# The next-to-last head's weights joined and split ahead of later casts, and loads reordered at two places of the output projection

## The chip, the cores and the metric

The kernel runs on one core of one Trainium2 chip. The metric is the device time of one execution in microseconds (us). The time before is 2003.12 us, the median of three runs (2003.05 to 2004.46).

## The reference

One block of a streaming encoder on 512 tokens of width 2048, all in float32. The input is normalised and projected; eight heads of stick-breaking attention and eight of forgetting attention follow; their normalised outputs go through `w_out` onto the residual, and then through a squared-ReLU layer of width 8192:

```python
h = rmsnorm(x, g_attn[l])
proj = jnp.einsum('bsd,de->bse', h, w_in[l])
...
o_sb = stick_breaking_attention(qa, ka, va)
o_fox = forgetting_attention(qf, kf, vf, log_f)
mixed = jnp.concatenate([head_rmsnorm(o_sb, g_out_sb[l]),
                         head_rmsnorm(o_fox, g_out_fox[l])], axis=-1)
x = x + jnp.einsum('bse,ed->bsd', mixed, w_out[l])
h2 = rmsnorm(x, g_mlp[l])
u = jax.nn.relu(jnp.einsum('bsd,df->bsf', h2, w_up[l]))
x = x + jnp.einsum('bsf,fd->bsd', u * u, w_down[l])
return rmsnorm(x, g_final)
```

Stick-breaking attention weighs key s for query t with `exp(log_beta + rest)`, where `rest` is a reversed running sum of `log_keep` along the keys.

## The kernel before

**Split operands.** Every float32 operand of a product is split in a high half (a cast to fp32r on ScalarE: `wh`, `hi`, `ph`, `g..H`) and a low half (source minus high half, on VectorE: `wl`, `lo`, `pl`). A product of two operands is three matmuls (`mm3`, lines 78 to 80): high times high, high times low, low times high. So each piece of weights that TensorE uses has been loaded (a DMA on SyncE's queue, SP), cast (ScalarE) and subtracted (VectorE). The raw pieces (`wraw`, `wo`) live in three buffers and the halves (`wh`, `wl`) in three more, `wx` in one more for a while (tile `px`). A load waits for the buffer that the low half of an earlier piece frees.

**Large products in seven.** The projection by `w_out`, like the others, is made of seven products of half the size, numbered 1 to 7, of sums and differences of blocks (`a_source`, line 1329, and `WeightSums`, line 1025, which writes those sums to DRAM as `wsums`, `wraws` and `whigh`). The second output block of stick-breaking heads is computed early, while the last head is still at work (class `Second`, line 1136).

**The attention's plan.** Up to line 1282 the order on TensorE, ScalarE and VectorE is written by hand: `plan.at(time, function)` collects steps, and `plan.run()` issues them in order of the planned time. The time is only a sorting key: each engine works its own list in order and waits where an operand is missing. The heads pass through a chain. For a stick-breaking head `plan_sb` (line 868) plans `start`, `soft`, `maxed`, `scan` (a running sum along the keys on VectorE, and the subtraction behind it, line 887) and `weights` (the exponential, line 890). The weights of all heads but the last are then turned by a DMA transpose (`halves` and `turn_halves`, lines 939 to 945), joined again (`join_halves`, line 947, on ScalarE, `pt`), and split (`t_high`, line 951, `ph`; `t_low`, line 955, `pl`) for the head's product with the values (`o`, line 965). The last head's weights are turned on TensorE (`turn`, line 931). The numbers for the next-to-last head stand in line 1260, those of the last head's scan in line 894, those of the pieces of `Second` in lines 1225 and 1226.

**The output projection.** From line 1594 on no times are given. The program is written piece by piece (`out_piece(p, db, m0)`: product p, column block db, rows m0 and m0 + 1), and the recording layer sorts the instructions of all engines by a simulated timeline; `with tc.issue_after(ins)` keeps what is written under it behind an instruction that it names. Around the change, in block 0, product 1 and product 4 come first (`accoa`, `accob`), then 5 (`accoc`), 6 (`accoa` again), 3 (`accoc` again) and 7 (`accoa`). When a product is complete, `take` (line 1547) adds it from PSUM to quarters of the residual (`x`, loaded by `begin`, line 1543); a complete quarter is stored (`xd`), transposed on TensorE (`turn_quarter`, line 1567, `tr`) and scaled by ScalarE into `hr` (line 1565). From `hr`, `left_form` (line 1588) makes the left operands `f` of the next layer, each with its sum on VectorE (lines 1335 to 1341), its cast and its low half. `hr` of column block 1 takes the buffers of block 0, so it is written once the forms of block 0 have been read. `pending` is the list of forms to come, one behind each piece.

Product 6's pieces load both halves ready-made (`whigh` and `wsums`, lines 1515 and 1516). Its last piece uses `wx`, the extra buffer. The loads for product 3's second piece, and the next quarter of the residual, are kept behind `behind`, a load of product 6 (lines 1632 and 1652).

Of the kernel before, what the change touches and what calls it, by code (L numbers as in the profile page):

```python
# [38 lines left out]
def block_kernel(ctx, tc, x, g_attn, w_in, b_f, g_out_sb, g_out_fox, w_out, g_mlp, w_up, w_down, g_final, y):  # L39
# [726 lines left out]
    with tc.tile_pool(name="att", bufs=1, side="right", reuse_waits="tile") as at, \  # L766
# [78 lines left out]
        class Head:  # L845
# [22 lines left out]
            def plan_sb(self, plan, t):  # L868
                g = self.h

                def start():
                    self.w = wide("w")
                    act.activation(self.w, self.s, AF.Abs)

                def soft():
                    act.activation(self.w, self.w, AF.Exp, scale=-1.0)
                    act.activation(self.w, self.w, AF.Ln, bias=1.0)

                def maxed():
                    dve.scalar_tensor_tensor(self.w, self.s, 0.0, self.w, op0=ALU.max, op1=ALU.add)  # L880
                    causal(self.w, ALU.is_gt, 0.0)

                def scan():
                    for r in rows(self.w):

                        dve.tensor_tensor_scan(r[:, ::-1], r[:, ::-1], r[:, ::-1], 0.0, op0=ALU.add, op1=ALU.max)
                    dve.tensor_tensor(self.w, self.s, self.w, op=ALU.subtract)

                def weights():
                    act.activation(self.w, self.w, AF.Exp)  # L890
                    causal(self.w, ALU.is_gt, 0.0)

                last_ = self.i == 2 * NH - 1
                for dt, f in zip((6.4, 7.7, 10.2, 14.5, 19.2) if last_ else (9.8, 11.0, 13.6, 17.0, 22.0), (start, soft, maxed, scan, weights)):
                    plan.at(t + dt, f)

            def plan_fox(self, plan, t):
# [52 lines left out]

            def t_high(self):
                self.ph, self.pl = wide("ph", F32R), wide("pl", F32R)
                act.copy(self.ph, self.pt)

            def t_low(self):
                dve.tensor_tensor(self.pl, self.pt, self.ph.bitcast(F32), op=ALU.subtract)
# [209 lines left out]
            sp.dma_start(second_x[db], xq[:, :2, db * NT:(db + 1) * NT])  # L1166

        def take_second(db, t):
            dve.tensor_tensor(second_x[db][:, t, :], second_x[db][:, t, :], second_ps[db][t], op=ALU.add)

        TRI, TPER = 0.681, 26.05
        heads = [Head(i) for i in range(2 * NH)]
# [7 lines left out]
        for n in range(2 * NH + 1):  # L1180
# [34 lines left out]
            else:  # L1215
# [4 lines left out]
                for db in range(2):  # L1220
                    for n0, m0 in enumerate((4, 6, 0, 2)):
                        w = Second(db, m0)
                        if db:
                            plan.at(t + (-10.0, -9.0, -8.0, 6.0)[n0], w.load)
                            plan.at(t + (3.4, 4.5, 10.3, 11.35)[n0], w.cast_apart if n0 < 2 else w.cast, *((n0,) if n0 < 2 else ()))
                            plan.at(t + (4.6, 7.0, 11.75, 12.95)[n0], w.low)
                        else:
                            plan.at(t + (-11.0, -5.5, -1.4, -1.35)[n0], w.load_parts)
                        for tt in range(2):
                            plan.at(t + at_unit16(unit), w.multiply, tt)  # L1230
                            unit += 1
# [25 lines left out]
            if 0 <= i_o < 2 * NH - 1:  # L1257
                H = heads[i_o]
                last_ = i_o == 2 * NH - 2
                for dt, f in zip((12.4, 15.5, 19.3) if last_ else (5.4, 8.5, 9.8), (H.join_halves, H.t_high, H.t_low)):  # L1260
                    plan.at(t + dt, f)
                if last_:
                    continue
# [331 lines left out]
    for db in range(2):  # L1595
# [3 lines left out]
        else:  # L1599
# [11 lines left out]
                out_piece(1, 0, 4)  # L1611
            begin(1, 0, 0)
            with tc.issue_after(last_heads[1].ins):
                for m0 in (0, 2, 4, 6):
                    ins = out_piece(4, 0, m0)
            for p in (1, 5):
                g_form(p, (6, 7), (7, 8))
# [5 lines left out]
        for p in (1, 5, 6, 3, 7, 4)[:6 if db else 5]:  # L1623
            for m0 in () if db == 0 and p == 1 else (0, 2, 4, 6):
# [22 lines left out]
                if (db or p in (3, 7, 4)) and m0 in (2, 6) and first_loads:  # L1647

                    with tc.issue_after(ins.ins):
                        u, k, a = first_loads.pop(0)  # L1650
                        units[u].load(k, a)
                if db == 0 and p == 6 and m0 == 4:
                    behind = ins

                    with tc.issue_after(ins.ins):
# [17 lines left out]
            if db == 1 or p != 1:  # L1673
                take(p, db)
            if db == 1:
                pending += [(q, 0, j) for q in {1: (4, 5, 6), 6: (2, 7, 3)}.get(p, ()) for j in range(2)]
            if len(squares) > 0:

                with ExitStack() as order_:
# [596 lines left out]
```

## Time and profile before

| what | value |
|---|---|
| median of three runs | 2003.12 us (2003.05 to 2004.46) |
| the profiled execution | 2002.29 us |
| its span, first to last instruction | 2000.6 us |
| TensorE busy | 99% of the span |
| VectorE busy | 88% |
| ScalarE busy | 60% |
| granted TensorE clock, mean | 0.999 |

The profile is of one execution, and times within it are in us from the start of its span. Busy time of TensorE is modelled, since matmuls overlap: the step from one 512-column matmul to the next is shorter than the duration that stands in its row. A row of the timeline gives the start, the duration, the engine (PE is TensorE, DVE VectorE, ACT ScalarE, POOL GpSimd, SPq SyncE's queue of DMA issues), the line, the operation, what it writes and reads, and in brackets the time that its engine sat idle before it, with the instruction that ended the wait. For a DMA the row is its issue; when it lands is told apart.

### The profile page before, as it was taken

To read this page: it belongs to the slowest core of one execution; us is meant where nothing else is said; L and a number is where in the kernel's file an instruction comes from. 1 tells how busy PE (TensorE), PEld (TensorE's weight loads), DVE (VectorE), ACT (ScalarE), POOL (GpSimd) and SP (SyncE) were. 2 spreads that over 40 slices of the span, in tenths; PEclk is the share of its full clock that TensorE was granted. 3 is DMA by queue.
4 is the path that set the end of the run, shared out by engine and by line. 5 is a ranking of instruction groups with operands and counts; after the bars stand their busy time and mean duration, and the time that the engine had idled before them with its cause. 6 is when DMAs were issued, how large, how long until landed. Compare 5 with 4: busy or idle time off the path is not lost.

```text
span 2000.6 us, 26669 instructions
## 1 busy us (share of the span) xinstructions
PE 1989.1 (99%) x10096; PEld 1708.7 (85%) x10096; DVE 1754.5 (88%) x1992; ACT 1205.0 (60%) x1636; POOL 63.1 (3%) x73
## 2 busy tenths in 40 slices
PE   9999999999999999999999999999999999999998
PEld 9988888888888889888888888888888888888887
DVE  7876888888888688999999999998898888988896
ACT  7544666778775565767677676766543444344344
POOL 0000011110110000000000000000000000000003
PEclk9999999999999999999999999999999999999999
DMA  7346977677786962666666666666694674674642
GB/s 258 126 146 203 285 247 232 201 227 222 218 295 223 325 216 95 200 207 197 220 187 211 203 197 203 199 212 232 243 351 166 231 270 145 238 271 162 217 161 85
DMA packets 309072, 426.66 MB, mean 213 GB/s; under 512 B 49440, under 2 KB 198736, under 8 KB 302416
## 3 DMA queue, kind: packets, MB, share of 16 engines
q1 hardware_dynamic: 307920, 422.33, 63.7%
q10 hardware_dynamic: 1024, 2.63, 0.3%
q8 instruction: 79, 1.29, 0.2%
q14 instruction: 49, 0.40, 0.1%
HBM read 318.07 MB, written 97.01 MB: 207 GB/s over the span
## 4 chain that ended last, share of the span: by engine, by line
PE 97%; DMA 1%; DVE 1%; issue 0%; ACT 0%; SPq 0%; DVEq 0%; ACTq 0%
PE psa L1415 11%; PE accd L79 8%; PE accd L80 8%; PE accd L78 8%; PE accq L78 6%; PE accq L79 6%; PE accq L80 6%; PE psa L1413 6%; PE psc L1415 5%; PE psc L1413 3%; PE psb L1415 3%; PE psb L1413 1%; PE m L79 1%; PE m L78 1%; PE m L80 1%; PE vy L79 1%
## 5 line engine op out<-in xcount | busy, mean ns | idle before, releaser
L2062 ACT CAST wh<-wd 128x1024 fp32r<-128x1024 f32 x126 | 125.0, 999 | 168.3 <-PE accd L80 58.2
L1948 DVE TENSOR_TENSOR wl<-wu,wh 128x1024 fp32r<-128x1024 f32 x157 | 191.4, 1220 | 13.4 <-ACT wh L1942 13.4
L78 PE MATMUL accq<-hH,wh 128*128 128x512 f32 x512 | 200.3, 391 | 0.0
L79 PE MATMUL accq<-hL,wh 128*128 128x512 f32 x512 | 199.4, 389 | 0.0
L80 PE MATMUL accq<-hH,wl 128*128 128x512 f32 x512 | 199.3, 389 | 0.0
L1942 ACT CAST wh<-wu 128x1024 fp32r<-128x1024 f32 x157 | 166.3, 1060 | 48.7 <-PE psc L1415 22.9
L1415 PE MATMUL psa<-f,wh 128*128 128x512 f32 x712 | 177.1, 391 | 0.0
L79 PE MATMUL accd<-wl,uf 128*128 128x512 f32 x436 | 169.6, 389 | 0.0
L80 PE MATMUL accd<-wh,uf 128*128 128x512 f32 x436 | 169.6, 389 | 0.0
L78 PE MATMUL accd<-wh,uf 128*128 128x512 f32 x436 | 169.4, 389 | 0.0
L2069 DVE TENSOR_TENSOR wl<-wd,wh 128x1024 fp32r<-128x1024 f32 x126 | 144.1, 1152 | 11.5 <-ACT wh L2062 11.5
L1415 PEld LDWEIGHTS psa<-f,wh 128*128 128x128 f32 x712 | 130.8, 188 | 25.3
L2062 ACT CAST wx<-wd 128x1024 fp32r<-128x1024 f32 (+1 forms) x82 | 80.8, 995 | 107.1 <-PE accd L80 43.5
L1783 DVE TENSOR_TENSOR m<-m,accd 128x1024 f32<-128x1024 f32 x84 | 102.3, 1218 | 47.4 <-PE accd L80 47.4
L80 PEld LDWEIGHTS accq<-hH,wl 128*128 128x128 f32 x512 | 96.1, 188 | 20.3
L78 PEld LDWEIGHTS accq<-hH,wh 128*128 128x128 f32 x512 | 96.2, 188 | 19.0
L79 PEld LDWEIGHTS accq<-hL,wh 128*128 128x128 f32 x512 | 96.2, 188 | 18.9
L78 PE MATMUL accd<-wx,uf 128*128 128x512 f32 x284 | 110.5, 389 | 0.0
L79 PE MATMUL accd<-wx,uf 128*128 128x512 f32 x284 | 110.5, 389 | 0.0
L80 PE MATMUL accd<-wx,uf 128*128 128x512 f32 x284 | 110.5, 389 | 0.0
L1413 PEld LDWEIGHTS psa<-f,wl 128*128 128x128 f32 x712 | 94.8, 191 | 5.2
L1413 PE MATMUL psa<-f,wl 128*128 128x256 f32 x712 | 97.2, 282 | 0.0
(498 smaller groups left out, 5069.3 us busy)
## 6 DMA issues: line engine op xcount, KB each, us to landing
wu<-in_w_up_dram SPq DMA_DIRECT2D x60, 1024.0 KB, 6.5
ufd<-st SPq DMA_DIRECT2D x98, 512.0 KB, 3.6
wd<-in_w_down_dram SPq DMA_DIRECT2D x48, 1024.0 KB, 8.4
uf<-ufd SPq DMA_DIRECT2D x42, 1024.0 KB, 6.6
wraw<-in_w_in_dram SPq DMA_DIRECT2D x64, 512.0 KB, 6.0
wo<-wsums SPq DMA_DIRECT2D x28, 512.0 KB, 4.8
wd<-in_w_down_dram SPq DMA_DIRECT2D x16, 768.0 KB, 8.0
uf<-ufd SPq DMA_DIRECT2D x14, 768.0 KB, 4.5
```

The lines of the kernel that those rows point to most:

```text
L78: pe.matmul(out, sh, mh, start=first, stop=False, skip_group_check=True)
L79: pe.matmul(out, sh, ml, start=False, stop=False, skip_group_check=True)
L80: return pe.matmul(out, sl, mh, start=False, stop=last, skip_group_check=True)
L1413: ins = pe.matmul(ps[:, 2 * P:], lo[:, a, :], f_parts(p, a)[0], start=False, stop=last, skip_group_check=True)
L1415: ins = pe.matmul(ps, hi[:, a, :], f_both(p, a), start=a == PAIRS[0] and p in (1, 5), stop=last, skip_group_check=True)
L1783: dve.tensor_tensor(M[p][:, :, db, :], M[p][:, :, db, :], ps, op=ALU.add)
L1942: act.copy(rooms[k][0], srcs[k])
L1948: lows[0] = dve.tensor_tensor(lo, srcs.pop(k), hi.bitcast(F32), op=ALU.subtract)
L2062: act.copy(rooms[k + 3][0], srcs[k + 3])
L2069: dve.tensor_tensor(rooms[k + 2][1], srcs.pop(k + 2), rooms[k + 2][0].bitcast(F32), op=ALU.subtract)
```

## The change

There are four parts; instructions are only moved, none is added or taken away.

1. In the attention's plan the subtraction behind the scan becomes a step of its own (`less`), which for the last head comes later than the scan (18.5 instead of 14.5). The next-to-last head's join, cast and low half come earlier (11.0, 14.0, 18.2 in place of 12.4, 15.5, 19.3). The cast and the low half of the last piece of `Second` come later (14.7 and 18.9 in place of 11.35 and 12.95).
2. The first piece of product 4 (`out_piece(4, 0, 0)`) is kept behind the next-to-last head's cast and behind the last `take_second` of block 0.
3. `behind` is the load of product 6's piece m0 = 6 instead of m0 = 4, so the quarter of the residual and product 3's second weights are loaded after product 6's last piece.
4. In the list of forms `(3, 0)` and `(7, 1)` change places.

```diff
                     for r in rows(self.w):
                         dve.tensor_tensor_scan(r[:, ::-1], r[:, ::-1], r[:, ::-1], 0.0, op0=ALU.add, op1=ALU.max)
+
+                def less():
                     dve.tensor_tensor(self.w, self.s, self.w, op=ALU.subtract)
...
-                for dt, f in zip((6.4, 7.7, 10.2, 14.5, 19.2) if last_ else (9.8, 11.0, 13.6, 17.0, 22.0), (start, soft, maxed, scan, weights)):
+                for dt, f in zip((6.4, 7.7, 10.2, 14.5, 18.5, 19.2) if last_ else (9.8, 11.0, 13.6, 17.0, 17.0, 22.0), (start, soft, maxed, scan, less, weights)):
                     plan.at(t + dt, f)
...
-                            plan.at(t + (3.4, 4.5, 10.3, 11.35)[n0], w.cast_apart if n0 < 2 else w.cast, *((n0,) if n0 < 2 else ()))
-                            plan.at(t + (4.6, 7.0, 11.75, 12.95)[n0], w.low)
+                            plan.at(t + (3.4, 4.5, 10.3, 14.7)[n0], w.cast_apart if n0 < 2 else w.cast, *((n0,) if n0 < 2 else ()))
+                            plan.at(t + (4.6, 7.0, 11.75, 18.9)[n0], w.low)
...
-                for dt, f in zip((12.4, 15.5, 19.3) if last_ else (5.4, 8.5, 9.8), (H.join_halves, H.t_high, H.t_low)):
+                for dt, f in zip((11.0, 14.0, 18.2) if last_ else (5.4, 8.5, 9.8), (H.join_halves, H.t_high, H.t_low)):
...
-                for m0 in (0, 2, 4, 6):
+                with tc.issue_after(now["t_high"].ins), tc.issue_after(now["second", 0].ins):
+                    out_piece(4, 0, 0)
+                for m0 in (2, 4, 6):
                     ins = out_piece(4, 0, m0)
...
-                if db == 0 and p == 6 and m0 == 4:
+                if db == 0 and p == 6 and m0 == 6:
                     behind = ins
...
-                pending += [(q, 0, j) for q in {1: (4, 5, 6), 6: (2, 7, 3)}.get(p, ()) for j in range(2)]
+                pending += {1: [(q, 0, j) for q in (4, 5, 6) for j in range(2)], 6: [(q, 0, j) for q, j in ((2, 0), (2, 1), (7, 0), (3, 0), (7, 1), (3, 1))]}.get(p, [])
```

(`now["t_high"]` and `now["second", db]` only record the two instructions that part 2 names.) Lines behind the first part move by two, those behind the third by four, in the changed kernel.

**Where the instructions stand.** VectorE at the end of the attention, before: `wl` are the low halves of the third and the fourth piece of `Second`, L886 the four scans of the last head, `wx` the first piece of product 4, L887 the subtraction, and `pl` the low half of the next-to-last head's weights.

```order
L180 TENSOR_TENSOR wl<-wraw,wh 128x1024 x2
L886 SCALAR_TENSOR_TENSOR w<-w 128x128
L886 SCALAR_TENSOR_TENSOR w<-w 128x256
L886 SCALAR_TENSOR_TENSOR w<-w 128x384
L886 SCALAR_TENSOR_TENSOR w<-w 128x512
L61 TENSOR_TENSOR wx<-wo,wx 128x1024
L887 TENSOR_TENSOR w<-s,w 128x1280
L956 TENSOR_TENSOR pl<-pt,ph 128x1280
```

The same place after the change (`pl` is L958 there, the subtraction L889, and L1171 is `take_second`):

```order
L180 TENSOR_TENSOR wl<-wraw,wh 128x1024
L886 SCALAR_TENSOR_TENSOR w<-w 128x128
L886 SCALAR_TENSOR_TENSOR w<-w 128x256
L886 SCALAR_TENSOR_TENSOR w<-w 128x384
L886 SCALAR_TENSOR_TENSOR w<-w 128x512
L958 TENSOR_TENSOR pl<-pt,ph 128x1280
L889 TENSOR_TENSOR w<-s,w 128x1280
L180 TENSOR_TENSOR wl<-wraw,wh 128x1024
L1171 TENSOR_TENSOR x_5278<-x_5278,acc_5260 128x512
L1171 TENSOR_TENSOR x_5278<-x_5278,acc_5261 128x512
L61 TENSOR_TENSOR wx<-wo,wx 128x1024
```

`pl` now follows the scans directly; the subtraction, the second `wl` and `wx` stand behind it. On ScalarE the join and the cast of `ph` move in the same way ahead of the second `wh` and of `wx`.

SyncE's queue of loads at the end of product 6, before: `wh` is the high half of its last piece but one, `wx` its last piece, `x` the next quarter of the residual, `xd` the store of a complete quarter, `wo` from `in_w_out_dram` the weights of product 3, `wo` from `wsums` those of product 7.

```order
L1515 DMA wh<-whigh 128x1024
L1545 DMA x_5878<-in_x_dram 128x2x512
L1534 DMA wo<-in_w_out_dram 128x2x512
L1574 DMA xd_5536<-x_5278 128x1024
L1534 DMA wo<-in_w_out_dram 128x2x512
L1515 DMA wx<-whigh 128x1024
L1516 DMA wx<-wsums 128x1024
L1534 DMA wo<-in_w_out_dram 128x2x512
L1536 DMA wo<-wsums 128x1024 x3
```

After (the lines are two higher):

```order
L1517 DMA wh<-whigh 128x1024
L1576 DMA xd_5536<-x_5278 128x1024
L1517 DMA wx<-whigh 128x1024
L1518 DMA wx<-wsums 128x1024
L1547 DMA x_5893<-in_x_dram 128x2x512
L1536 DMA wo<-in_w_out_dram 128x2x512 x3
L1369 DMA wu<-in_w_up_dram 128x2x256 x2
L1538 DMA wo<-wsums 128x1024 x2
```

The two halves of `wx` now go out ahead of `x` and of product 3's weights, and two loads for the next layer (`wu`) come ahead of product 7's weights.

TensorE at the same place, before, with buffer numbers (`wh_5903` is the first piece of product 3, `wh_5927` its second, `wx` the last piece of product 6):

```order
L79 MATMUL accoc_5551<-wl_5904,g3_5521 128x512
L80 MATMUL accoc_5551<-wh_5903,g3_5522 128x512
L78 MATMUL accoc_5551<-wh_5927,g3_5521 128x512
L78 MATMUL accoa_5549<-wx_5880,g6_5517 128x512
L79 MATMUL accoc_5551<-wl_5928,g3_5521 128x512
```

After:

```order
L80 MATMUL accoa_5549<-wh_5862,g6_5518 128x512
L78 MATMUL accoc_5551<-wh_5903,g3_5521 128x512
L78 MATMUL accoa_5549<-wx_5878,g6_5517 128x512
L79 MATMUL accoa_5549<-wx_5878,g6_5517 128x512
L80 MATMUL accoa_5549<-wx_5878,g6_5518 128x512
```

The twelve matmuls of `wx` stood in two parts, one and eleven, among those of product 3's second and third piece; now they are one block behind the first matmul of product 3. Product 3's low half (`L79 accoc`) comes only when the block is done. On VectorE the `take` of product 6 (L1552, L1554 in the changed kernel) moves with it, from behind four low halves of products 3 and 7 to a place ahead of them. At the forms, the transposes of one quarter (`tr`, twice four), which had twelve matmuls between them, now follow each other directly.

More of the change, by code (lines that the diff above doesn't have):

```diff
@@ L952, in t_high @@
                 self.ph, self.pl = wide("ph", F32R), wide("pl", F32R)
-                act.copy(self.ph, self.pt)
+                now["t_high"] = act.copy(self.ph, self.pt)
             def t_low(self):
@@ L1168, in take_second @@
         def take_second(db, t):
-            dve.tensor_tensor(second_x[db][:, t, :], second_x[db][:, t, :], second_ps[db][t], op=ALU.add)
+            now["second", db] = dve.tensor_tensor(second_x[db][:, t, :], second_x[db][:, t, :], second_ps[db][t], op=ALU.add)
         TRI, TPER = 0.681, 26.05
```

## Prediction

> **What bounds the kernel now.** The page's first part gives busy time, share of the span and instructions; this is its row of engines:
>
> ```profile
> PE 1989.1 (99%) x10096; PEld 1708.7 (85%) x10096; DVE 1754.5 (88%) x1992; ACT 1205.0 (60%) x1636; POOL 63.1 (3%) x73
> ```
>
> TensorE is busy 1989.1 us of a span of 2000.6 us, so a change of order can win no more than its waits. The view of who waited for whom, for TensorE alone, has besides the program's start these three (total, times, longest):
>
> ```profile
> PE o L79 <- DVE pl L956: 1.5, 1, 1.5
> PE tr L1559 <- ACT hr L1565: 0.6, 1, 0.6
> PE accoa L78 <- DMA wx<-whigh: 0.3, 1, 0.3
> ```
>
> These, 2.4 us together, are the three places that the change touches: the product of the next-to-last head, the last piece of product 6, and the transposes in front of the residual's forms. 0.2% of this kernel, about what a measurement of it can tell from no change, is 4.0 us. So the three waits together are worth less than can be told, and the question is how much of them goes and what new waits come.
>
> The first place, in order of time. TensorE (start, duration, line, operands, idle time before):
>
> ```profile
> 602.62 0.28 PE L78 MATMUL o<-ph,vh 128*128 128x256 f32 x1
> 604.41 0.39 PE L79 MATMUL o<-pl,vh 128*128 128x256 f32 x1 [1.51 <-DVE pl L956]
> ```
>
> `ph` is there, `pl` is not: the low half is 1.51 us late. Where it was held up stands on ScalarE and VectorE:
>
> ```profile
> 592.34 1.03 ACT L173 CAST wh<-wraw 128x1024 fp32r<-128x1024 f32 x1
> 595.25 1.05 ACT L173 CAST wh<-wraw 128x1024 fp32r<-128x1024 f32 x1 [1.87 <-PE acc L80]
> 596.20 3.14 ACT L949 COPY pt<-pl 128x2560 uint16<-128x2560 uint16 x1
> 599.17 1.07 ACT L60 CAST wx<-wo 128x1024 fp32r<-128x1024 f32 x1
> 600.11 1.29 ACT L953 CAST ph<-pt 128x1280 fp32r<-128x1280 f32 x1
> ```
>
> ```profile
> 596.33 1.23 DVE L180 TENSOR_TENSOR wl<-wraw,wh 128x1024 fp32r<-128x1024 f32 x1 [1.18 <-ACT wh L173]
> 597.47 2.97 DVE L886 TENSOR_TENSOR_SCAN w<-w 128x128 f32<-128x128 f32 x4
> 600.35 1.20 DVE L61 TENSOR_TENSOR wx<-wo,wx 128x1024 fp32r<-128x1024 f32 x1
> 601.47 1.49 DVE L887 TENSOR_TENSOR w<-s,w 128x1280 f32<-128x1280 f32 x1
> 602.87 1.48 DVE L956 TENSOR_TENSOR pl<-pt,ph 128x1280 fp32r<-128x1280 f32 x1
> ```
>
> ScalarE waits 1.87 us in front of the second `wh` cast, and the join (L949) stands behind it though it needs nothing from it. VectorE then does `wx` and the subtraction L887 ahead of `pl`.
>
> **The change, step by step.** *Joined and split earlier.* When the joined halves can start is set by the DMA transpose that brings them; its issue row, and its line's time from issue to landing (min, median, max of 15):
>
> ```profile
> 583.90 6.81 SPq L945 DMA_TRANSPOSE pl<-pt  x1
> ```
>
> ```profile
> DMA to landing us min/median/max: 4.1/4.1/7.1
> ```
>
> Even with the longest landing it is there at 583.90 + 7.1 = 591.0. The join now follows the first `wh` cast: it starts at 592.34 + 1.03 = 593.4, ends at 596.5 (3.14), and `ph` is done at 597.8 (1.29). On VectorE the scan no longer stands behind the second `wl`; it waits for GpSimd's mask on the same tile:
>
> ```profile
> 594.08 1.69 POOL L837 TENSOR_SCALAR_AFFINE_SELECT w<-w 128x256 f32<-128x256 f32 x2 [13.12 <-DVE w L880]
> ```
>
> That is done at 595.8, so the scan ends at 595.8 + 2.97 = 598.8 and `pl`, now right behind it, at 598.8 + 1.48 = 600.3. TensorE asks for it at 604.41 − 1.51 = 602.9. Cover 2.6 us, so the whole 1.51 us goes. Behind it: the subtraction L887 ends at 600.3 + 1.49 = 601.8, earlier than its 602.96 now, so the exponentials, the mask and the turn of the last head are not later. The second `wl` moves from 596.33 to 601.8 and ends at 603.0; it is wanted by the piece behind the product,
>
> ```profile
> 606.27 0.45 PE L78 MATMUL acc<-wh,g 128*128 128x512 f32 x1
> ```
>
> which moves to 606.27 − 1.51 = 604.8: cover 1.8 us. `wx`, done last, is a weight of product 4, behind pieces of product 1. The term is −1.51 us. The splitting off of the subtraction as a step of its own changes no other head's order: nothing.
>
> *Loads behind product 6's last piece.* TensorE's rows there (product 3 begins in `accoc`, and product 6's last piece, `wx`, runs one piece later), and the load queue:
>
> ```profile
> 654.71 0.39 PE L78 MATMUL accoc<-wh,g 128*128 128x512 f32 x1
> 654.94 0.39 PE L79 MATMUL accoc<-wl,g 128*128 128x512 f32 x1
> ```
>
> ```profile
> 658.13 0.50 PE L78 MATMUL accoa<-wx,g 128*128 128x512 f32 x1 [0.31 <-DMA wx<-whigh]
> ```
>
> ```profile
> 643.54 0.38 SPq L1515 DMA_DIRECT2D wh<-whigh  x1
> 643.98 0.42 SPq L1545 DMA_DIRECT2D x<-in_x_dram  x1
> 644.45 0.46 SPq L1534 DMA_DIRECT2D wo<-in_w_out_dram  x1
> 645.01 0.84 SPq L1574 DMA_DIRECT2D xd<-x  x1
> 645.95 0.62 SPq L1534 DMA_DIRECT2D wo<-in_w_out_dram  x1
> 646.66 0.92 SPq L1515 DMA_DIRECT2D wx<-whigh  x1
> 647.63 0.68 SPq L1516 DMA_DIRECT2D wx<-wsums  x1
> ```
>
> Landing after issue (of the group of issues by operands, KB each, us):
>
> ```profile
> x<-in_x_dram SPq DMA_DIRECT2D x1, 512.0 KB, 8.3
> ```
>
> ```profile
> wx<-whigh SPq DMA_DIRECT2D x1, 512.0 KB, 11.4
> ```
>
> `x` lands at 643.98 + 8.3 = 652.3, the first half of `wx` at 646.66 + 11.4 = 658.1: four transfers of 512 KB further on, 1.45 us each. They drain one after the other, so a place in the queue is a time. In the new order `xd` takes the place of `x`, and `wx`'s halves the next two: 652.3 + 1.45 = 653.7 and 655.2; then `x` at 656.6 and product 3's second weights at 658.1. The queue's backlog starts with loads that wait for TensorE, so all of this comes 1.51 us earlier too: 652.2, 653.7, 655.1, 656.6.
>
> Now TensorE: product 6's last twelve matmuls follow the first matmul of product 3 directly. Their first wants the high half at 654.94 − 1.51 = 653.4 (there since 652.2), their second, 0.23 us on (the step between the two rows), the low half at 653.7 (it lands at 653.7). No cover. Twelve matmuls take 12 × 0.23 = 2.7 us. VectorE now has `take` of product 6 ahead of the low halves of product 3, so `wl` of its second piece waits for the end of product 6 (656.2) and for `x` (655.1); `take` is done at about 657.5, the weights land at 656.6, are cast by 657.7 (1.05 as at L173) and are low by 658.9 (1.23); TensorE asks for them at 653.2 + 24 × 0.23 + 0.2 = 658.9. No cover either. So the old 0.31 us goes and about 0.3 us of new waits come, for two needs that come out even; the bounds are 0 (all lands half a transfer earlier) and 1.5 us (each need is one transfer late once; a second lateness of the same chain hides behind the first). I take 0.3, near the lower end, since the row of `wx` shows the transfers on time to 0.3 us now.
>
> [...]
>
> ```profile
> 628.00:630.00 2.00, 2.00 (x10) 1.67 (x9) 2.00 (x3) 0.46 (x1) 0.00 (x0) 1.00 0.38 61
> 652.00:654.00 2.00, 2.00 (x10) 1.68 (x9) 2.00 (x3) 0.09 (x1) 0.00 (x0) 1.00 1.05 381
> ```
>
> (share of the DMA engines and GB/s are the last two columns). [...]
>
> *Behind it.* Product 7's first weights go into the buffer that the second `wl` of product 3 frees. Today:
>
> ```profile
> 657.37 0.32 SPq L1536 DMA_DIRECT2D wo<-wsums  x1
> ```
>
> ```profile
> 661.97 1.05 ACT L60 CAST wh<-wo 128x1024 fp32r<-128x1024 f32 x1 [0.19 <-DMA wo<-wsums]
> ```
>
> Issued at 657.37, landed at 661.97: 4.6 us. Now they are issued when `wl` ends, 658.9, also behind two loads of `wu`; they land at 663.5, and are cast and low at 663.5 + 1.05 + 1.23 = 665.8. TensorE reaches them after product 6's twelve and product 3's 48 matmuls: 653.2 + 60 × 0.23 = 667.0. Cover 1.2 us: nothing.
>
> *Two forms of the residual change places.* The rows:
>
> ```profile
> 731.74 1.05 ACT L60 CAST wh<-wo 128x1024 fp32r<-128x1024 f32 x1 [1.68 <-DMA wo<-wsums]
> 732.70 1.56 ACT L1565 ACTIVATE hr<-tr,g_rest 128x256 f32<-128x256 f32 x4
> ```
>
> ```profile
> 733.58 0.66 PE L1559 MATMUL tr<-ident,x 128*128 128x128 f32 x4 [0.59 <-ACT hr L1565]
> 733.99 0.47 PE L79 MATMUL accob<-wl,g 128*128 128x512 f32 x1
> ```
>
> The swap lets the first half of `hr` be overwritten earlier, but L1565 runs right behind a cast that itself waited 1.68 us for a load: it doesn't wait for `hr`, so it comes no earlier. But the second four transposes now follow the first four directly instead of twelve matmuls later. They need the second PSUM buffer, which the last two of the four L1565 free at 732.70 + 1.56 = 734.3; the first four are through at 733.99. New wait 0.3 us on top of 0.59. Bounds: −0.59 (should L1565 come earlier after all) and 0.78 (half of 1.56, if both buffers come in turn).
>
> **The sum.** −1.51 − 0.31 + 0.3 + 0.3 = −1.2 us against the profiled execution. That one took 2002.29 us, 1.69 us more than its span, and stands 0.83 us under the median 2003.12 of the three runs. Carried to the median: 2001.9 us.
>
> **Rivals.** *Given back at the seam.* If the backlog of loads, which fills the queue for 25 us, keeps its old times instead of moving with TensorE, the low half of `wx` lands at 655.2 for a need at 653.7: 1.5 us, and the third term is 1.5 in place of 0.3. Then 2003.12 − 1.51 − 0.31 + 1.5 + 0.3 = 2003.1. For it: the queue is full (1.05 at 652). Against: it is not full at 628 (0.38), and what fills it waits for TensorE's buffers.
>
> *Slower: product 7's loads come late.* They are issued 3 us later relative to TensorE than today, through one chain (take of product 6, low half, buffer, load). It decides from a landing of 4.6 + 1.2 = 5.8 us on. With the 8.3 us of the `x` row they land at 667.2, are low at 669.5 and TensorE waits 2.5 us: 2001.9 + 2.5 = 2004.4. With the 11.4 us of the longest row it waits 5.6: 2007.5, which could be told from no change. For it: such landings happen where the queue is full. Against: by then what stood in the queue has drained.
>
> *The change doesn't do what it says.* If the join still ends no earlier (its transpose lands later than the longest row), the first term is 0: 2003.12 − 0.31 + 0.6 = 2003.4. Against: 2.4 us between 591.0 and 593.4.
>
> **How the numbers follow.** Forecast 0.64, given back 0.20, product 7 late 0.08, no effect 0.08. Low end: all three waits gone and none new, 2003.12 − 2.41 = 2000.7. High end: the forecast's terms at their worst, −1.82 + 1.5 + 0.78 = +0.5, so 2003.6; this holds the second and the fourth case. The third stays out. Faster by over 0.2% would be under 1999.1, more than the waits hold: 0.02, for what I cannot see. Slower by over 0.2%, over 2007.1, is the far end of the third case: 0.03. The rest, 0.95, is within.
>
> **What would show it.** TensorE's waits without `o` <- `pl`; the join at 593 to 594, `pl` by 601; `wx`'s loads issued by 646 and landed by 654; product 6's last twelve in one block with under 0.5 us of idle; the second four transposes with some 0.3 us. It is wrong if a wait over 1 us stands in products 3 or 7, or at the forms, or if TensorE's waits are the same in total.

## The result, and the profile after

| | before | after |
|---|---|---|
| median of 22 runs each | 2003.74 us | 2000.94 us |
| lowest and highest | 2001.80, 2006.90 | 1999.39, 2002.51 |
| the profiled execution | 2002.29 us | 2002.51 us |
| its span | 2000.6 us | 2000.8 us |

The ratio is 0.9984 with a 95% interval of 0.9977 to 0.9990: some 3 us, where 1.2 were forecast (the medians differ by 2.8). Two things stand out. The runs of the kernel before scatter over 5 us, those of the changed kernel over 3. And the two profiled executions do not show the gain at all: that of the kernel before was nearly its fastest run, that of the changed kernel its slowest. So the two traces tell where waits went, and not how large they usually are.

TensorE's waits in the changed kernel (total, times, longest). The wait of `o` for `pl` is gone, that for the transposes has doubled:

```profile
PE vx L306 <- DVE still L302: 1.6, 1, 1.6
PE tr L1561 <- ACT hr L1567: 1.2, 1, 1.2
PE accoa L79 <- DMA wx<-wsums: 0.4, 1, 0.4
```

The first place, on ScalarE, VectorE and TensorE. Everything here is 0.8 us later than in the trace of the kernel before (the first row's cast stood at 592.34 there). That was lost at the start: the record of the granted clock begins with full clock at 9.87 us here and at 6.86 there, and from 12 us on up to this place every matmul stands 0.81 to 0.85 us later. So this pair of traces hides the gain: the 1.5 us that `o` no longer waits are made up for by these 0.8 us, by 0.6 us more of waiting at the transposes and by 0.3 us in their block.

```profile
593.16 1.03 ACT L173 CAST wh<-wraw 128x1024 fp32r<-128x1024 f32 x1
594.09 3.12 ACT L951 COPY pt<-pl 128x2560 uint16<-128x2560 uint16 x1
597.24 1.26 ACT L955 CAST ph<-pt 128x1280 fp32r<-128x1280 f32 x1
598.41 1.05 ACT L173 CAST wh<-wraw 128x1024 fp32r<-128x1024 f32 x1
```

```profile
596.26 3.15 DVE L886 TENSOR_TENSOR_SCAN w<-w 128x128 f32<-128x128 f32 x4 [0.30 <-POOL w L837]
599.34 1.46 DVE L958 TENSOR_TENSOR pl<-pt,ph 128x1280 fp32r<-128x1280 f32 x1
600.72 1.48 DVE L889 TENSOR_TENSOR w<-s,w 128x1280 f32<-128x1280 f32 x1
```

```profile
603.44 0.28 PE L78 MATMUL o<-ph,vh 128*128 128x256 f32 x1
603.55 0.28 PE L79 MATMUL o<-pl,vh 128*128 128x256 f32 x1
```

The join stands directly behind the first cast, `pl` is done at 600.8 and wanted at 603.5: the cover of 2.6 us that was forecast is 2.7. At the seam of products 6 and 3, the twelve matmuls run in one block, and the low half comes a little late:

```profile
654.16 0.39 PE L78 MATMUL accoa<-wx,g 128*128 128x512 f32 x1
654.97 0.50 PE L79 MATMUL accoa<-wx,g 128*128 128x512 f32 x1 [0.41 <-DMA wx<-wsums]
```

At the transposes, TensorE and ScalarE:

```profile
733.56 1.39 PE L1561 MATMUL tr<-ident,x 128*128 128x128 f32 x8 [1.23 <-ACT hr L1567]
```

```profile
731.72 1.05 ACT L60 CAST wh<-wo 128x1024 fp32r<-128x1024 f32 x1 [2.29 <-DMA wo<-wsums]
732.67 1.56 ACT L1567 ACTIVATE hr<-tr,g_rest 128x256 f32<-128x256 f32 x4
```

The cast and L1567 stand at the same time after the start as before (731.74 and 732.70), to 0.03 us. TensorE came 0.66 us earlier and waited that much longer.

### The profile page after: what moved, and what is told of

Its sections match the earlier page's. It is cut to its first block, busy times and chain, and to the rows that moved or that the text cites. A ratio compares the mean times of both kernels' runs of the same rounds, so it can differ in the third digit from the quotient of the medians.

```text
span 2000.8 us, 26665 instructions
## 1 busy us (share of the span) xinstructions
PE 1990.3 (99%) x10096; PEld 1709.8 (85%) x10096; DVE 1754.7 (88%) x1992; ACT 1205.5 (60%) x1636; POOL 63.1 (3%) x73
## 4 chain that ended last, share of the span: by engine, by line
PE 98%; DMA 1%; DVE 1%; ACT 0%; issue 0%; DVEq 0%; SPq 0%; ACTq 0%
PE psa L1417 11%; PE accd L80 8%; PE accd L78 8%; PE accd L79 8%; PE accq L78 6%; PE accq L80 6%; PE accq L79 6%; PE psa L1415 6%; PE psc L1417 5%; PE psc L1415 3%; PE psb L1417 3%; PE psb L1415 1%; PE m L80 1%; PE m L79 1%; PE m L78 1%; PE vy L80 1%
## 5 line engine op out<-in xcount | busy, mean ns | idle before, releaser
L79 PE MATMUL accq<-hL,wh 128*128 128x512 f32 x512 | 199.4, 389 | 0.0
L80 PE MATMUL accq<-hH,wl 128*128 128x512 f32 x512 | 199.3, 389 | 0.0
L79 PE MATMUL accd<-wl,uf 128*128 128x512 f32 x436 | 169.6, 389 | 0.0
L80 PE MATMUL accd<-wh,uf 128*128 128x512 f32 x436 | 169.6, 389 | 0.0
L80 PEld LDWEIGHTS accq<-hH,wl 128*128 128x128 f32 x512 | 96.1, 188 | 20.3
L79 PEld LDWEIGHTS accq<-hL,wh 128*128 128x128 f32 x512 | 96.2, 188 | 18.9
L79 PE MATMUL accd<-wx,uf 128*128 128x512 f32 x284 | 110.5, 389 | 0.0
L80 PE MATMUL accd<-wx,uf 128*128 128x512 f32 x284 | 110.5, 389 | 0.0
```

What stands on the lines that cost most here:

```text
L79: pe.matmul(out, sh, ml, start=False, stop=False, skip_group_check=True)
L80: return pe.matmul(out, sl, mh, start=False, stop=last, skip_group_check=True)
```

## The experiments

Times are medians; each ratio is to runs of the kernel before on the same chip, with its 95% interval. 0.5 and 1.00 are the granted TensorE clock. "Half clock" below is a stretch at 0.5.

**The parts alone.** e1: parts 1 and 2 of the change alone (`less`, join, cast, low half, `out_piece(4, 0, 0)`); e2: part 3 alone; e3: part 4 alone; e4: the whole change again. The edits of e2 and of e3 against the kernel before (e1 has the other lines of the change's diff):

```diff
-                if db == 0 and p == 6 and m0 == 4:
+                if db == 0 and p == 6 and m0 == 6:
```

```diff
-                pending += [(q, 0, j) for q in {1: (4, 5, 6), 6: (2, 7, 3)}.get(p, ()) for j in range(2)]
+                pending += {1: [(q, 0, j) for q in (4, 5, 6) for j in range(2)], 6: [(q, 0, j) for q, j in ((2, 0), (2, 1), (7, 0), (3, 0), (7, 1), (3, 1))]}.get(p, [])
```

> The kernel before with only the next-to-last head's join, split and the later cast moved (the forms and the loads of product 6 as before). By the prediction's first term: 1.5 us under the kernel before, the wait of o for pl gone, the waits at product 6 (0.3) and at the transposes (0.6) as they were. By the rival that the loads of the second weights set the time of the transposes at 733 (there the changed kernel started at 733.56 and the kernel before at 733.58, though TensorE came 0.67 us earlier): the 1.5 us goes into a longer wait at the transposes, and the time falls by under 0.8 us.

> The kernel before with only product 6's last loads put behind its last piece, so that its last twelve matmuls run in one block. By the prediction's second and third terms: no change within 0.3 us. By the rival that the one profile of the kernel before (2002.29 us, 1.45 us under the median of its 22 runs) shows this wait smaller than most runs have it: 1 us or more under the kernel before, and in the trace of a kernel that keeps the old place a wait for wx well over 0.31 us.

> The kernel before with only two entries of the list of left forms exchanged. By the prediction's fourth term: 0.3 us slower. By the trace of the changed kernel, where the wait at the transposes is 1.23 us in place of 0.59 and the block after them ends 0.25 us later on the clock: 0.3 to 0.9 us slower. By the rival that this part brings what the sum lacks (1.6 us between the forecast of 1.2 and the measured 2.8): faster by over 1 us.

> The changed kernel itself once more, for a second trace. If the waits of its first trace are typical: o waits for nothing, product 6 waits 0.4 us, the transposes 1.2 us, and the start is as late as there; if that run (2002.51 us, the slowest of its 22) was an unlucky one, one of these is smaller by about 1 us. The time should be 2 to 3.5 us under the kernel before; the three parts alone should add up to it if they don't depend on each other.

| run | median of 11, lowest, highest | ratio (interval) |
|---|---|---|
| e1, heads alone | 2000.60 (2000.31 to 2002.36) | 0.9985 (0.9976 to 0.9994) |
| e2, loads alone | 2004.24 (2000.35 to 2006.70) | 0.9998 (0.9990 to 1.0007) |
| e3, forms alone | 2005.18 (2002.23 to 2008.38) | 1.0002 (0.9993 to 1.0012) |
| e4, all | 2000.55 (1999.51 to 2001.88) | 0.9985 (0.9976 to 0.9993) |
| kernel before, 33 runs | 2003.56 (2001.83 to 2009.38) | |

The heads' part is the whole gain, 3.0 us, twice what was forecast for it, and it alone narrows the scatter. Neither theory had that number. By the ratios e2 is 0.4 us faster and e3 0.4 us slower, each with an interval of some 1.8 us to either side, so neither alone tells its expectations apart; with e1 they add up to e4. In e4's own trace the waits are near those of the first trace of the changed kernel (0.8 us for `wx`, 1.2 at the transposes). The rival that the transposes swallow e1's gain falls: they start at 731.84 there and not at 733, though part of its mechanism shows in the trace (the wait there is 1.0 us):

```profile
PE tr L1561 <- ACT hr L1567: 1.0, 1, 1.0
```

Where the other 1.5 us come from is seen in the trace of e3, which still has the old order of the heads. TensorE, behind its wait:

```profile
605.87 0.39 PE L79 MATMUL o<-pl,vh 128*128 128x256 f32 x1 [2.10 <-DVE pl L956]
...
608.72 0.63 PE L79 MATMUL acc<-wl,g 128*128 128x512 f32 x1
609.15 0.63 PE L80 MATMUL acc<-wh,g 128*128 128x512 f32 x1
609.57 0.63 PE L78 MATMUL acc<-wh,g 128*128 128x512 f32 x1
```

The step from one matmul to the next is 0.43 us instead of 0.23. The table by stretches says why (the columns are the sum, busy time of PE, PEld, DVE, ACT and POOL, then the granted clock, the DMA share, GB/s):

```profile
606.00:608.00 2.00, 2.00 (x14) 2.00 (x14) 1.01 (x2) 0.00 (x0) 0.75 (x2) 0.79 1.04 424
608.00:610.00 2.00, 2.00 (x6) 1.61 (x6) 0.00 (x0) 1.57 (x3) 0.00 (x0) 0.50 0.26 104
610.00:612.00 2.00, 2.00 (x14) 1.81 (x13) 0.69 (x1) 0.01 (x1) 0.00 (x0) 0.85 0.00 0
```

After a wait of 2.1 us the clock is halved, from 607.17 to 610.58 by its record, 3.41 us. From the row of `o` above to the first matmul into `accoa` it is 7.35 us here and 5.78 in the kernel before, so the stretch costs 1.6 us. TensorE counts as busy all the while. So this wait of 2.1 us cost 1.6 us more than it lasted, and no row of waits shows it.

**Which wait holds the second cast.** e5 is the kernel before with the load of that cast issued from ScalarE, ahead of the end of the transposing DMA:

```diff
-                            plan.at(t + (-10.0, -9.0, -8.0, 6.0)[n0], w.load)
+                            plan.at(t + (-10.0, -9.0, -8.0, 7.0)[n0], w.load if n0 < 3 else w.load_act)
...
+            def load_act(self):
+                self.raw = wp.tile([P, self.a, self.b], F32, tag="wraw", name="wraw")
+                act.dma_start(self.raw, self.src)
```

> The kernel before with one load moved: the weights of the second cast ahead of the join are issued from ScalarE's queue behind L873 (at about 589.8) instead of from SyncE behind the transposing DMA (at 590.8, 591.6 and 592.2 in three traces of this order). Theory: this load holds the cast, and with it the join, ph, the scan and pl. In those three traces issue plus landing (590.81 + 4.4, 591.56 + 4.2, 592.15 + 4.5) is the start of the cast within 0.1 us, and o starts 9.16 us after the cast in each. Then the cast starts at about 594.3, the wait of o is about 0.6 us in place of 1.4 to 2.1, and the time falls to 2000.8 to 2001.5 with the narrow spread of the kernels with the new order. Rival: the cast waits for TensorE's product L80, as the profile of the kernel before names it; then neither the wait nor the time changes (2003.6, spread 2002 to 2009).

2005.51 us (2002.36 to 2007.59), ratio 1.0002 (0.9993 to 1.0011). The forecast time was missed by 4 us. The issue on ScalarE's queue, the line's time to landing, the transposing DMA and the cast:

```profile
588.67 0.39 ACTq L1150 DMA_DIRECT2D wraw<-in_w_out_dram  x1
```

```profile
DMA to landing us min/median/max: 9.4/9.4/9.4
```

```profile
584.19 8.05 SPq L945 DMA_TRANSPOSE pl<-pt  x1
```

```profile
598.13 1.05 ACT L173 CAST wh<-wraw 128x1024 fp32r<-128x1024 f32 x1 [4.73 <-PE acc L80]
```

```profile
607.29 0.58 PE L79 MATMUL o<-pl,vh 128*128 128x256 f32 x1 [2.59 <-DVE pl L956]
```

The load was issued 2 us earlier but took 9.4 us in place of 4.4, beside the transpose: 588.67 + 9.4 = 598.1, where the cast starts. TensorE reached `o` at 602.89, 0.3 us later than before (602.62), so it wasn't TensorE that held the cast 2.9 us longer: the rival falls, and the name "PE acc L80" in the profile's row is a wrong one. And `o` starts 9.16 us after the cast, as in every trace of the old order. What fell is the sum of the expectation: in this trace the load that was in flight beside the transpose landed no earlier, and the transpose itself took 8.05 us.

**How much a wait costs.** e6 and e7 are the changed kernel with the old order of `less`, and `pl` made three times over in e6, four times in e7 (the same values), so that it is late by a fixed time. The edit of e6:

```diff
-                for dt, f in zip((6.4, 7.7, 10.2, 14.5, 18.5, 19.2) if last_ else (9.8, 11.0, 13.6, 17.0, 17.0, 22.0), (start, soft, maxed, scan, less, weights)):
+                for dt, f in zip((6.4, 7.7, 10.2, 14.5, 14.5, 19.2) if last_ else (9.8, 11.0, 13.6, 17.0, 17.0, 22.0), (start, soft, maxed, scan, less, weights)):
...
-                dve.tensor_tensor(self.pl, self.pt, self.ph.bitcast(F32), op=ALU.subtract)
+                for _ in range(3 if self.i == 2 * NH - 2 else 1):
+                    dve.tensor_tensor(self.pl, self.pt, self.ph.bitcast(F32), op=ALU.subtract)
```

> The changed kernel with the last head's subtraction put ahead of pl again and the subtraction that makes pl done three times over (the same values). pl is then late by a fixed amount: the last of the three ends at 600.74 + 2 x 1.40 + 1.46 = 605.0 on the clock of the changed kernel's trace, where TensorE asks at 603.5, so TensorE waits about 1.5 us, as in the trace of the kernel before, but the same in every run. Theory (the time lost is the wait, and from a wait somewhere between 1.5 and 2.1 us on also a stretch of 3.41 us at half clock): 1.5 us over the changed kernel, 2002.0 to 2002.3, narrow spread, no stretch at 0.5 in the granted clock. Rival (any wait of this kind also costs clock): 3 us or more over it.

> The same with the subtraction done four times: a wait of about 2.9 us in every run. Theory: 2.9 us for the wait and 1.5 to 1.7 us for one stretch of 3.41 us at half clock right behind it (in some runs none, where the wait is split over two of the clock's intervals): 4.4 to 4.6 us over the changed kernel in most runs, about 2005.1, and 0.5 in the granted clock behind the product. Rival (only the wait counts): 2.9 us over it, 2003.5, the clock at 1.00 throughout.

e6 has 2002.94 us (2002.13 to 2004.82), e7 2005.69 us (2003.63 to 2006.59). The waits came out longer than meant, since the repeated subtractions step by 1.6 us (three take 4.76 us in e6) and not by 1.40, so e6 passed the bound that it was meant to stay under:

```profile
605.10 0.39 PE L79 MATMUL o<-pl,vh 128*128 128x256 f32 x1 [2.10 <-DVE pl L959]
```

```profile
606.15 0.39 PE L79 MATMUL o<-pl,vh 128*128 128x256 f32 x1 [3.42 <-DVE pl L959]
```

The stretch behind the wait, in e6 and in e7:

```profile
606.00:608.00 2.00, 2.00 (x11) 2.00 (x9) 2.00 (x4) 0.00 (x0) 0.00 (x0) 0.50 0.83 223
```

```profile
606.00:608.00 2.00, 1.84 (x14) 1.85 (x15) 2.00 (x4) 0.00 (x0) 0.00 (x0) 1.00 1.02 418
```

The shorter wait brought half clock in its profiled execution, the longer one not. The record of the clock explains it: its changes lie whole multiples of 3.413 us from the first (583 such steps from 6.86 to 1996.84 us in the kernel before, 582 from 9.87 to 1996.43 in the changed kernel), and in the traces below full and half clock part by the idle time inside one such interval (the borders are worked out from these changes). In e6, all 2.10 us lay in one (602.04 to 605.45). In e7 the idle time lay across the border at 604.56, 1.83 us ahead of it and 1.60 behind. The runs fit: in e7, nine of eleven stand at 2004.9 to 2006.6 and two at 2003.6 and 2003.9, that is about 3.4 us of wait over the changed kernel's 2000.7, with the 1.6 of e3 for the clock or without. In e6, eight stand at 2002.1 to 2003.1 and three at 2003.8 to 2004.8. The rivals (a wait always costs clock; only the wait counts) both fall. All traces in which `o` waits:

| trace | idle in one interval, at most | clock behind it |
|---|---|---|
| before | 1.30 | full |
| e2 | 1.39 | full |
| e15 | 1.53 | full |
| e16 | 1.80 | full |
| e7 | 1.83 | full |
| e6 | 2.10 | half |
| e3 | 2.10 | half |
| e5 | 2.13 | half, for two intervals |
| e14 | 2.34 | half |
| e13 | 2.59 | half |

In e5, where `o` waits 1.42 us for `ph` and then 2.59 for `pl`, 1.87 us of the idle time lie in the second interval, and the clock stays at half for it too (6.83 us in all). In the eight traces where `o` waits for nothing, no interval but those at the start and the end has more than 1.33 us, and the clock stays full.

**The kernel before, four times more.** The trace of 1.51 us was one sample; e13 to e16 are four more of the unchanged kernel.

> The kernel before, traced again (the first of four such looks). Theory: the time of an execution is about 2000.6 us (the kernel with the heads' part alone, whose o waits for nothing) plus the wait of o, plus 1.6 us for each stretch of 3.41 us at half clock right behind it, within 1 us; the wait is 9.16 us less the time from the start of the second wh cast to TensorE's arrival at pl; that cast starts when its load lands, which SyncE issues when the transposing DMA is through; and there is a stretch at half clock where more than about 2 us of the wait lie in one of the clock's intervals of 3.41 us (1.83 us did not do it, 2.10 us did). Mean wait over the four looks: 2 us or more. Rival (the trace of 1.5 us is typical, and the rest comes from elsewhere): waits of 1.3 to 1.7 us in all, and time lost at another place.

> The second of the four looks at the kernel before, with what was said for the first: a time of 2000.6 us plus the wait of o plus 1.6 us for each stretch at half clock, and a wait that follows the landing of the second wh cast's load.

> The third of the four looks at the kernel before, with what was said for the first: a time of 2000.6 us plus the wait of o plus 1.6 us for each stretch at half clock, and a wait that follows the landing of the second wh cast's load.

> The fourth of the four looks at the kernel before, with what was said for the first: a time of 2000.6 us plus the wait of o plus 1.6 us for each stretch at half clock, and a wait that follows the landing of the second wh cast's load.

Of e13 the two rows of SyncE, the cast and `o`:

```profile
584.41 7.66 SPq L945 DMA_TRANSPOSE pl<-pt  x1
592.17 0.52 SPq L166 DMA_DIRECT2D wraw<-in_w_out_dram  x1
```

```profile
596.56 1.05 ACT L173 CAST wh<-wraw 128x1024 fp32r<-128x1024 f32 x1 [2.98 <-issue]
```

```profile
605.72 0.38 PE L79 MATMUL o<-pl,vh 128*128 128x256 f32 x1 [2.59 <-DVE pl L956]
```

and all traces with the old order of the heads and of that load:

| trace | transpose holds SyncE | load issued | cast starts | `o` goes on | wait | half clock | time |
|---|---|---|---|---|---|---|---|
| before | 6.81 | 590.81 | 595.25 | 604.41 | 1.51 | no | 2002.29 |
| e2 | 7.09 | 591.56 | 595.81 | 604.97 | 1.39 | no | 2003.43 |
| e3 | 7.32 | 592.15 | 596.70 | 605.87 | 2.10 | yes | 2005.38 |
| e16 | 7.43 | 591.18 | 595.67 | 604.83 | 2.38 | no | 2002.73 |
| e14 | 7.63 | 591.83 | 596.13 | 605.29 | 2.34 | yes | 2006.10 |
| e13 | 7.66 | 592.17 | 596.56 | 605.72 | 2.59 | yes | 2006.13 |
| e15 | 8.08 | 592.42 | 596.83 | 605.99 | 2.58 | no | 2004.62 |

From issue to cast it is 4.25 to 4.55 us in all, from cast to `o` 9.16 or 9.17: the wait is set for the most part by how long the transpose holds SyncE's queue. The trace that the forecast was read from has the shortest transpose of the seven. The last four executions have a mean wait of 2.47 us, and two of the four have half clock; that is the theory's side, and the rival (1.3 to 1.7 us) falls. What the theory said of the time (2000.6 us, the wait, 1.6 us for half clock, within 1 us) held for e16 alone (2003.0, measured 2002.73); e13, e14 and e15 are 1.3, 1.6 and 1.4 us over it. Part of that stands in the two later waits, those for `wx` and for the transposes: 1.7, 2.3 and 1.5 us in these, 1.0 us in e1. Another 0.1 to 0.35 us was lost at the start, as in the first trace of the changed kernel. The rest, 0.2 to 0.7 us, stays open.

**The smaller parts, on the narrow base.** e8 is the changed kernel without part 3, e10 without part 4, e12 without both (e1 again), e9 the changed kernel again; e9 to e12 ran beside each other.

> The changed kernel with product 6's last loads back at their old place: the heads' part and the forms' part together. The traces with the heads' part alone and with the whole change differ at two places: product 6 waits 0.0 without the loads' part and 0.4 and 0.8 with it, the transposes 1.0 without the forms' part and 1.2 with it. If these waits are all: 0.4 to 0.8 us under the changed kernel, 2000.0. If product 6's wait is hidden by the later wait for the loads at the transposes: the same as the changed kernel, 2000.6.

> The changed kernel once more, beside the next three on one chip, since parts worth a few tenths of a us are to be told apart. 2000.5 to 2001.0, and a third trace: o waits for nothing, product 6 about 0.4 to 0.8, the transposes about 1.2.

> The changed kernel with the two left forms back in their old order. The prediction's fourth term says the exchange costs 0.3 us: this is then 0.3 us under the changed kernel. The rival is that the exchange, by putting eight transposes in one block, gains or costs nothing that shows, since the weights that TensorE multiplies next are clocked by their loads: the same within 0.3 us.

> The heads' part alone, beside the changed kernel on one chip: by the first comparison (2000.60 and 2000.55) the two are the same within 0.3 us, and all of the change's gain is this part; by the prediction's terms the others cost 0.3 us together.

| run | median of 11, lowest, highest | ratio (interval) |
|---|---|---|
| e8, heads and forms | 2001.23 (2000.40 to 2001.99) | 0.9987 (0.9979 to 0.9996) |
| e9, all | 2000.68 (1999.74 to 2001.46) | 0.9982 (0.9973 to 0.9991) |
| e10, heads and loads | 2000.72 (1999.49 to 2001.87) | 0.9982 (0.9973 to 0.9991) |
| e12, heads | 2001.16 (2000.45 to 2002.56) | 0.9986 (0.9977 to 0.9994) |

The forms' part does nothing that shows (e10 against e9, 0.04 us). e8 gained nothing where its expectation, read from single traces once more, had up to 0.8 us; its own trace had the longest wait for `wx` of all:

```profile
PE accoa L78 <- DMA wx<-whigh: 1.5, 1, 1.5
```

Over all traces the wait at product 6 is 0 to 1.5 us with the old place of the loads (ten traces, mean 0.6) and 0 to 0.8 with the new one (eight, mean 0.3). Heads alone against the whole change: 22 runs with a median of 2001.16 and 22 with 2000.65 (e1 and e12, e4 and e9); the difference of 0.5 us has an interval (by resampling the runs) of -0.35 to 1.2. Whether the loads' part gains those tenths stays open.

**A faster version.** e11 is the changed kernel with the four L1567 ahead of the cast that waits for its load:

```diff
-            act.mul(hr[db][j][:, a, i, t0 * 2 * P:(t0 + 1) * 2 * P], tr[:, i, :], g_up[:, k:k + 1])
+            now["mul", t0, j, db] = act.mul(hr[db][j][:, a, i, t0 * 2 * P:(t0 + 1) * 2 * P], tr[:, i, :], g_up[:, k:k + 1])
...
+                    if db == 1 and p == 7 and m0 == 6:
+                        order_.enter_context(tc.issue_after(now["mul", 0, 0, 1].ins))
                     ins = out_piece(p, db, m0)
```

> The changed kernel with the four L1567 that free the PSUM tiles of the transposes put ahead of the cast they stand behind (the third piece's weights of product 7, which waits 2.3 us for its load; two instructions of VectorE about 15 us later change places with it). If the wait at the transposes is made by this order, as the prediction's fourth term says, the 1.2 us there goes, and TensorE then waits for the low half of that cast (734.0 on the clock of the changed kernel's trace, where it would ask at 733.4): 0.5 to 0.7 us under the changed kernel, about 2000.0. If the loads clock this stretch altogether, the wait moves to wl and the time stays the same.

1999.92 us (1999.23 to 2000.67), ratio 0.9981 (0.9972 to 0.9989); beside e9 it is 0.76 us less (interval by resampling 0.08 to 1.31). ScalarE, and TensorE without a wait:

```profile
728.27 1.57 ACT L1567 ACTIVATE hr<-tr,g_rest 128x256 f32<-128x256 f32 x4
729.91 1.05 ACT L60 CAST wh<-wo 128x1024 fp32r<-128x1024 f32 x1
```

```profile
731.09 1.04 PE L1561 MATMUL tr<-ident,x 128*128 128x128 f32 x8
```

It has the lowest median of all kernels here. The gain is what was forecast if the order on ScalarE makes the wait, though its interval begins just above zero. The trace alone would not show it: the load had landed when the cast's turn came, and in e10, with the old order on ScalarE, TensorE waits for nothing there either.

## Why the prediction was partly wrong, point by point

- **"A change of order can win no more than its waits".** This failed: the medians differ by 2.8 us, more than the 2.41 on which the low end of its range rests. After waits that put 2.10 us or more into one interval of its clock (e3, e6, e13, e14) TensorE ran at half clock for 3.41 us, in e5 for 6.83, and counted as busy. Of the 99 runs of the kernel before that were made beside e1, e5 and e9, 29 have a mean granted clock of 0.998 or less and all of these take 2004.3 us or more; that is the least number with half clock, since e13 has such a stretch and a mean of 0.999; of 99 runs with the new order of the heads (after, e1, e4, e8 to e12) none has so low a mean, and none takes more than 2002.6. The trace of the kernel before happened to have no such stretch.
- **Term 1, -1.51 us.** The mechanism was right: the join goes first, `pl` has a cover of 2.7 us (2.6 forecast), the second low half and the last head's subtraction are in time, nothing came in place of the wait. The size was wrong: 3.0 us in e1. The row of 1.51 us was taken as what every execution waits; the five traces of the kernel before have 1.51, 2.38, 2.34, 2.59 and 2.58, mean 2.28 (2.13 with e2 and e3, which keep this order). With half clock in at least 29 of 99 runs at 1.6 us, at least 0.5 in the mean, that makes 2.6 to 2.8, or more. The prediction noted that its trace stood under the median of the runs and then carried the term over unchanged: a trace faster than the median is one whose waits may be short.
- **What held `pl` up.** The prediction saw the second cast's wait of 1.87 us and took the name beside it (a matmul) as it stood. It was a load behind the transposing DMA (e5 and the table of seven traces), and that is what varies from run to run.
- **"Even with the longest landing it is there at 591.0".** Wrong by up to 3 us. The 7.1 us are the landing of the first head's transpose, issued at 216.9 us, which held SyncE for 5.04 us; for the last one, held 6.81, the profile has no landing. In e1 the join waits for the transpose until 9.98 us after its issue.

```profile
593.94 3.14 ACT L951 COPY pt<-pl 128x2560 uint16<-128x2560 uint16 x1 [0.64 <-DMA pl<-pt]
```

  It cost nothing, because `pl` has its 2.7 us. The rival "the change doesn't do what it says" was nearer than it looked.
- **Terms 2 and 3, -0.31 + 0.3.** The new wait was 0.41 us in the trace after and 0.3 in the mean of eight traces, as forecast; the old one was 0.6 in the mean of ten and not 0.31. The rival "given back at the seam" did not come. The low half of `wx` landed at 654.9, 0.4 us later than forecast on this execution's clock. Of the two needs that were to come out even, only that for `wx` was late. Product 7 waits for nothing, as forecast.
- **Term 4, +0.3.** The two sentences behind it held in the trace: L1567 comes no earlier, and the block of eight takes 1.39 us, against 1.04 in e11, so 0.35 us inside it. What was missed is that the first wait ends when a load lands and not some time after TensorE comes: in the trace after TensorE came earlier and waited 1.23 us. By the prediction's own test, a wait over 1 us at the forms, that step is wrong. In medians the exchange costs nothing (e10), and the wait varies with the load: 0.7 us in e9.
- **The chances.** That it would stay within 0.2% was right, the measured gain is 0.16%. It had 0.02 for a gain of over 0.2%, "more than the waits hold". The gain stayed under that and is still more than the waits of its trace: of the 1.5 us that term 1 lacked, 0.6 to 0.8 is the longer mean wait, at least 0.5 is half clock, and up to 0.4 stays open.

## What to carry to other kernels

A wait in one trace is one sample: where the runs scatter to one side and the trace lies at their low end, ask what sets the length of the wait (here a DMA ahead in the same queue) and cost the term by the scatter. The waits of TensorE that had 2.10 us or more in one interval of its clock cost some 1.6 us beyond their length here (e3, e6, e13, e14), and the order that gives `pl` 2.7 us of cover won 3.0 us (e1) where the trace showed a wait of 1.51. And an instruction that only frees a buffer shouldn't stand behind one that waits for a load (0.76 us in e11).

## What the runs showed of the hardware

The same DMA transpose held SyncE's queue for about 2.5 us in thirteen of the fourteen earlier heads, for 5.0 us in the first and for 6.8 to 8.1 us, by fifteen traces, in the last one, right behind four loads of 512 KB (whether these make it slow wasn't tried); the kernel before, line L945 (least, median and most in ns):

```profile
L945 SPq DMA_TRANSPOSE pl<-pt x15: 2485/2550/6806, 216.9 to 583.9; - x15
```

The load behind it on that queue was issued 0.10 or 0.11 us after it let the queue go, in all seven traces of the table, and a load beside it on another queue took 9.4 us in place of 4.4 (e5). In the ten traces in which `o` waits, half clock went with the idle time inside one interval of a grid of 3.413 us: at 1.83 us and less the clock stayed full, at 2.10 and more it was halved, for about 1.6 us of lost time (7.33 to 7.35 us from `o` to `accoa` in e3, e6, e13 and e14, 5.78 in the kernel before, e7, e15 and e16).
